# The recurrent mixer of a two-layer trunk: an order given by hand on a grid of twelve products, gated tiles through DRAM

## The chip, the cores and the metric

The kernel runs on one core of one Trainium2 chip. The metric is the device time of one execution in microseconds; of three runs the median is told. The engines go by TensorE (PE), VectorE (DVE), ScalarE (ACT), GpSimd (POOL) and SyncE (SP, whose queue issues most of the DMAs).

## The reference, cut to what matters

Two layers over 1024 frames of width 1024, fp32. Layer 0 is the one that the change touches: a recurrent mixer and its residual.

```python
def recurrent_mixer(hn, w_in, conv_w, conv_b, gate_a_w, ..., lam, w_out):
    z = hn @ w_in                                   # 1024 -> 2 x 1408
    gate, xr = jnp.split(z, 2, axis=-1)
    xr = causal_depthwise_conv(xr, conv_w, conv_b)  # width 4
    y = rg_lru(xr, ...)                             # 16 blocks of 88
    return (y * jax.nn.gelu(gate)) @ w_out          # 1408 -> 1024

# rg_lru, per block of 88 channels:
r = sigmoid(x @ w_a + b_a);  i = sigmoid(x @ w_x + b_x)
log_a = -8 * r * softplus(-lam);  a = exp(log_a)
h[t] = a[t] * h[t-1] + sqrt(1 - a[t]**2) * (i * x)[t]
```

Behind it come a squared-ReLU MLP, one shared key and value, chunked attention and a second MLP. Ahead of each product stands an RMS norm with a scale and shift that are computed from a condition vector (the modulation columns).

## The kernel before, in words

Every fp32 product is made of three: operands are split into a high half (ACT copies to fp32r) and a low half (DVE subtracts), and `mm3` (L272) issues high x high, high x low, low x high into one PSUM bank of 128x512. There are eight banks, taken in turn, and the frames go in two halves of 512. A product below is the whole sum into one bank: 24 matmuls of a unit of w_in, 3 for a gate of a block, 9 or 12 for one of W_out.

`Stream` (L66 to L244) brings the weights. It has one list of items in the order of use; `load` (L129) issues their DMAs on SP into a ring of seven tiles `ws`, `step` (L171) splits them into `wh` (L185, ACT) and `wl` (L189, DVE), and `done` gives them back. An item "u" is no weight but rows for a modulation column (L306, DVE). When `timed` is set, as it is in the MLPs alone, the low halves are put on a list and issued by `flush`.

The mixer has 11 channel tiles t of 128 (1408 in all) and 16 blocks b of 88, so that a block may lie across two tiles and `_done(t)` are the blocks that tile t completes. For each tile there are:

- a unit of w_in for the gate: 48 matmuls, Gelu on ACT (`gate_out`, L675);
- a unit of w_in for the channel: 48 matmuls, two ACT copies out of PSUM (`xr_out`, L680), the convolution as three DVE steps (`conv`, L691), and copies on SP that gather the blocks (L697);
- for each block `split_x` (high L278 on ACT, low L279 on DVE) and `lru`: 12 matmuls, four Sigmoids (L728), Tanh (L735), Sqrt (L737), Exp (L739), each with ACT table loads, DVE steps (L741 to L745), the scan (L746) and copies on SP to the tile `ym` (L750);
- the product with the gate (L709), and later the split of the gated tile into the moving operand of W_out (`split_yg`, L754).

W_out goes in three chunks c of 3, 4 and 4 gated tiles. `chunk2` (L562) makes the two products e of a unit j and half; an eviction on DVE (L571) adds them to the residual h. In the last chunk `tail` (L611) first does all first halves, then the second halves, and among these the norm of the first half for the MLP: squares (L450 on ACT, L451 on DVE), their sums over channels and 1/sqrt (`mm`), the broadcast (`bc`) and the modulation `mod` (L512 on DVE for several channel tiles, then L515 and L523 on ACT for each, and the low, L526, on DVE). Its eight results are the moving operands of the MLP's first products.

What sets the order: the opening (L761 to L862, the norm and the first three units) and each MLP stand in `tc.manual_schedule()`, so that each engine has the order of the code. All of the mixer between them (L865 to L962) is placed by the scheduler with its own estimate of times. Each engine works through its queue in order, and the queue of SP does so too: a DMA that waits for its source or for a free `ws` holds all behind it.

Of the kernel before, what the change touches and what calls it, by code (L numbers as in the profile page):

```python
# [65 lines left out]
class Stream:  # L66
# [8 lines left out]
    def __init__(self, nc, slot, wh, ws):  # L75
        self.nc, self.slot, self.wh, self.ws, self.ns = nc, slot, wh, ws, 7
        self.items = []
        self.loaded = self.raw = self.ring = self.pos = self.now = 0
        self.queue = {"p": [], "w": [], "a": [], "u": []}
        self.live = {"w": 0, "a": 0, "u": 0}  # L80
        self.cap = {"w": 8, "a": 0, "u": 3}

        self.lag = {"p": 4, "w": 0, "a": 2, "u": 4}
        self.hold = None
        self.timed = False
        self.los = []

    def item(self, loads, parts, to="w", rows=128, raw=True, after=None, use=None):

        it = dict(loads=loads, parts=parts, to=to, rows=rows, raw=raw, after=after, use=use,
                  n=len(self.items), at=0, op=[], left=1 if use else len(parts), need=[],
                  cost=sum(1 if one else 2 for _, _, one in parts))
        self.items.append(it)
        self.queue[to].append(it)
        return it
# [31 lines left out]
    def load(self, most=None):  # L129
        while self.loaded < (len(self.items) if self.hold is None else self.hold):  # L130
            it = self.items[self.loaded]
            if most is not None and it["n"] >= most:
                return
            if it["raw"]:
# [36 lines left out]
    def step(self, it):  # L171
        if it["use"]:
            it["use"](it["need"][0]["st"] if it["raw"] is None else it["st"])
        else:
# [13 lines left out]
            def low():  # L188
# [3 lines left out]
                it["hi"], it["lo"] = it["op"][0]  # L192

# [5 lines left out]
        it["left"] -= 1  # L199
        if not it["left"]:  # L200
            if it["raw"]:
                self.raw -= 1
                self.ring -= it["ring"]
            elif it["raw"] is False:
                self.live["u"] -= 1
# [42 lines left out]
def trunk(ctx: ExitStack, tc: tile.TileContext, I, out, dbg=None, stop=None):  # L248
# [92 lines left out]
    for t in range(12):  # L341
        if t < NT:
            for u in (t, 11 + t) if t < NT - 1 else (11 + t, t):
                ws.add(I["w_in"][u], 1024)
        some(2 if 2 < t < 7 else 0)
        if 1 < t < NT:
            for b in _done(t - 1) if t > 2 else (0, 1):
                if b % 4 == 0:
                    ws.add(I["gates"][b // 4], 8 * BLK)
    for c in range(3):  # L350
        kn = 4 if c else 3
        for j in range(4):
# [209 lines left out]
    def chunk2(it, kn, j, half, gh, gl, g, h):  # L562

        for e in range(2):
            m = 2 * j + e
            ps = bank()
            for k in range(kn):
                c = slice(k * 256 + e * 128, k * 256 + e * 128 + 128)
                mm3(ps, it["hi"][:, c], it["lo"][:, c], gh[k][:, hs(half)], gl[k][:, hs(half)],
                    k == 0, k == kn - 1)  # L570
            V.scalar_tensor_tensor(out=h[m][:, hs(half)], in0=ps, scalar=g[:, m : m + 1],  # L571
                                   in1=h[m][:, hs(half)], op0=ALU.mult, op1=ALU.add)
        return [2 * j, 2 * j + 1]

# [73 lines left out]

    xt = [slot() for _ in range(KD)]
# [23 lines left out]
    xc, xb, yg, ym, xraw = {}, {}, {}, {}, {}  # L673

    def gate_out(t, half, ps):  # L675
        if half == 0:
            yg[t] = slot()
        A_.activation(out=yg[t][:, hs(half)], in_=ps, func=AF.Gelu_apprx_tanh)

    def xr_out(t, half, ps):  # L680

        if half == 0:
            xraw[t], xc[t] = slot(), slot()
        A_.activation(out=xraw[t][:, hs(half)], in_=ps, func=AF.Copy)
        A_.activation(out=xc[t][:, hs(half)], in_=ps, func=AF.Identity,
                      scale=vc("cw", 3 * NT + t), bias=vc("cb", t))

    def conv(t):
        xr, y = xraw.pop(t), xc[t]
        for d in (1, 2, 3):  # L690
            V.scalar_tensor_tensor(out=y[:, d:], in0=xr[:, : S - d],  # L691
                                   scalar=vc("cw", (3 - d) * NT + t), in1=y[:, d:],
                                   op0=ALU.mult, op1=ALU.add)
        for b in _done(t):
            x = slot()
            for u, ps, bs in _pieces(b):
                nc.sync.dma_start(x[bs], xc[u][ps])  # L697
            xb[b] = x

    def split_x(b):  # L700
        hi, lo = slot(F32R), slot(F32R)
        split(xb[b][:BLK], hi[:BLK], lo[:BLK])
        xb[b] = (xb[b], hi, lo)

    late = []

    def flush(us):
        for u in us:
            V.tensor_tensor(out=yg[u], in0=yg[u], in1=ym[u], op=ALU.mult)  # L709

    gunit = [None]

    def lru(bs):

        R = {}
        for b in bs:
            if b % 4 == 0:
                gunit[0] = ws.next()
            it = gunit[0]
            x, xh, xl = (a[:BLK] for a in xb.pop(b))  # L720
            r, i_ = slot()[:BLK], slot()[:BLK]
            for gi, (dst, bias) in enumerate(((r, "gab"), (i_, "gxb"))):
                o = ((b % 4) * 2 + gi) * BLK
                w, wl = it["hi"][:BLK, o : o + BLK], it["lo"][:BLK, o : o + BLK]
                for half in range(2):
                    ps = bank()[:BLK]
                    mm3(ps, w, wl, xh[:, hs(half)], xl[:, hs(half)], True, True)
                    A_.activation(out=dst[:, hs(half)], in_=ps, func=AF.Sigmoid,  # L728
                                  bias=vc(bias, b)[:BLK])
            if b % 4 == 3:  # L730
                ws.done(it)
            R[b] = (r, i_, x, slot()[:BLK], slot()[:BLK])

        for b, (r, i_, x, tau, v) in R.items():
            A_.activation(out=tau, in_=r, func=AF.Tanh, scale=n4[:BLK, b : b + 1])  # L735
        for b, (r, i_, x, tau, v) in R.items():
            A_.activation(out=v, in_=tau, func=AF.Sqrt)  # L737
        for b, (r, i_, x, tau, v) in R.items():
            A_.activation(out=r, in_=r, func=AF.Exp, scale=n8[:BLK, b : b + 1])  # L739
        for b, (r, i_, x, tau, v) in R.items():  # L740
            V.scalar_tensor_tensor(out=v, in0=r, scalar=1.0, in1=v, op0=ALU.add, op1=ALU.mult)  # L741
            V.scalar_tensor_tensor(out=r, in0=r, scalar=1.0, in1=tau, op0=ALU.add, op1=ALU.mult)
            V.tensor_scalar(out=r, in0=r, scalar1=-1.0, scalar2=1.0, op0=ALU.mult, op1=ALU.add)
            V.tensor_tensor(out=i_, in0=i_, in1=x, op=ALU.mult)
            V.tensor_tensor(out=v, in0=v, in1=i_, op=ALU.mult)  # L745
            V.tensor_tensor_scan(out=tau, data0=r, data1=v, initial=0.0, op0=ALU.mult, op1=ALU.add)  # L746
            for u, ps, bs in _pieces(b):
                if u not in ym:
                    ym[u] = slot()
                nc.sync.dma_start(ym[u][ps], tau[bs])  # L750
                if ps.stop == 128:
                    late.append(u)

    def split_yg(k):  # L754
        a, b = slot(F32R), slot(F32R)
        split(yg[k], a, b)
        return a, b

    with tc.manual_schedule():  # L761
        n1 = Norm(xt, aa[:, 0:8], mods[0][:, 0:8])
        for k in range(KD):
            n1.sq(k, hs(0))
        sgm = slot()
        A_.activation(out=sgm, in_=cb, func=AF.Sigmoid)

        def ada_k(k):
            for j in (1, 0):
                ada_use(mods[0][:, j * 8 + k : j * 8 + k + 1], vc("ab0", j * 8 + k))(st.pop(0))  # L770
            gain(0, mods[0], 1, vc("n1g0", k), k, 1)

        def sq_b(*ks):
            for k in ks:
                n1.sq(k, hs(1))

        def normed(half, *ks):
            for k in ks:
                V.tensor_tensor(out=xt[k][:, hs(half)], in0=xt[k][:, hs(half)],
                                in1=n1.r[:, hs(half)], op=ALU.mult)  # L780

        def moded(k, half):
            if n1.hh[k] is None:
                n1.hh[k], n1.hl[k] = slot(F32R), slot(F32R)
            t, hi = (a[k][:, hs(half)] for a in (xt, n1.hh))
            A_.activation(out=t, in_=t, func=AF.Identity, scale=n1.a[:, k : k + 1],
                          bias=n1.sh[:, k : k + 1])
            A_.activation(out=hi, in_=t, func=AF.Copy)

        def lows(k, half):  # L790
            t, hi, lo = (a[k][:, hs(half)] for a in (xt, n1.hh, n1.hl))
# [841 lines left out]
```

## Time and profile before

| what | value |
|---|---|
| median of three runs | 2452.64 us (2448.2 to 2452.74) |
| the profiled execution's own time | 2450.6 us |
| its span | 2448.8 us |
| mean granted TensorE clock | 0.978 |
| busy: PE, DVE, ACT, POOL | 2304.2, 1759.7, 1258.3, 370.8 us |
| DMA | 351.91 MB, 144 GB/s on the mean |

The opening ends at about 78 us and the mixer at about 527 us of the span; MLP 0 begins there. Rows of the timeline are: start and duration in us, engine, line of the source, operation, out<-in, shape, and in brackets the idle time ahead of it with what ended it. Rows of groups have the busy time, the mean in ns of one, and the idle time before.

### The profile page before, as it was taken

How to read it: one execution, taken by the hardware profiler on the slowest of the kernel's cores; microseconds unless marked ns; L12 is line 12 of the kernel's file. 1: busy time of each engine (PE TensorE's matmuls, PEld its weight loads, DVE VectorE, ACT ScalarE, POOL GpSimd, SP SyncE). 2: the span in 40 equal slices, each digit the busy share in tenths (PEclk: the TensorE clock that was granted, in tenths of full speed). 3: DMA queues.
4: the chain of work that ended last, by engine and by line, in shares of the span. 5: the costliest groups of instructions: out<-in, count | busy, mean ns of one | idle time of the engine just before them, and what ended most of it. 6: DMA issues, size and time to landing. Idle time of an engine off the chain costs nothing.

```text
span 2448.8 us, 31664 instructions
## 1 busy us (share of the span) xinstructions
PE 2304.2 (94%) x11740; PEld 1941.3 (79%) x11740; DVE 1759.7 (72%) x2586; ACT 1258.3 (51%) x2054; POOL 370.8 (15%) x367
## 2 busy tenths in 40 slices
PE   5989887999999989999999999999999999999999
PEld 3767665777777867888899998998877888778887
DVE  7777777778777687778575466999367656777875
ACT  5577765356444553344343216999156555633442
POOL 0000000000000013332000026886000000023322
PEclk9989887999999999999999999999999999999999
DMA  8422355224566685546343300002413444774543
GB/s 299 129 76 81 113 157 193 64 78 156 207 217 215 233 294 185 155 142 200 114 145 123 113 5 12 10 19 80 142 48 125 156 175 177 259 260 145 159 144 141
DMA packets 138058, 351.91 MB, mean 144 GB/s; under 512 B 14160, under 2 KB 16336, under 8 KB 137904
## 3 DMA queue, kind: packets, MB, share of 16 engines
q1 hardware_dynamic: 114080, 278.45, 35.2%
q10 hardware_dynamic: 23824, 71.44, 7.6%
q8 instruction: 92, 1.51, 0.3%
q14 instruction: 62, 0.51, 0.1%
HBM read 254.42 MB, written 83.89 MB: 138 GB/s over the span
## 4 chain that ended last, share of the span: by engine, by line
PE 55%; DVE 17%; ACT 14%; DMA 8%; issue 5%; POOL 1%; SPq 0%; ACTq 0%; DVEq 0%; POOLq 0%
PE b L274 17%; PE b L275 17%; PE b L273 17%; DMA ws<-in_w_dram 2%; ACT wh L185 2%; DMA ws<-in_ada_dram 2%; DVE wl L189 2%; DVE s L306 2%; DMA hid<-s 1%; PE b L1439 1%; ACT s L1409 1%; DVE s L189 1%; POOL ws L121 1%; DVE ws L121 1%; ACT s L278 1%
## 5 line engine op out<-in xcount | busy, mean ns | idle before, releaser
L273 PE MATMUL b<-s,wh 128*128 128x512 f32 x2532 | 999.3, 398 | 57.4 <-DVE s L1101 15.3
L274 PE MATMUL b<-s,wh 128*128 128x512 f32 x2532 | 1003.3, 397 | 41.1 <-DVE s L279 37.6
L275 PE MATMUL b<-s,wl 128*128 128x512 f32 (+1 forms) x2296 | 909.0, 396 | 6.3 <-DVE wl L189 6.3
L273 PEld LDWEIGHTS b<-s,wh 128*128 128x128 f32 x2532 | 480.1, 190 | 184.8 <-DVE s L1079 19.6
L274 PEld LDWEIGHTS b<-s,wh 128*128 128x128 f32 x2532 | 482.2, 190 | 150.8 <-DVE s L279 41.5
L275 PEld LDWEIGHTS b<-s,wl 128*128 128x128 f32 (+1 forms) x2296 | 437.4, 191 | 105.2 <-DVE wl L189 8.5
L185 ACT ACTIVATE wh<-ws 128x1024 fp32r<-128x1024 f32 (+1 forms) x302 | 290.7, 971 | 428.6 <-POOL ws L121 263.3
L189 DVE TENSOR_TENSOR wl<-ws,wh 128x1024 fp32r<-128x1024 f32 (+1 forms) x249 | 305.3, 1228 | 149.4 <-ACT wh L185 147.1
L121 POOL TENSOR_TENSOR ws<-ws 128x512 f32<-128x512 f32 x21 | 28.2, 1341 | 1592.0 <-DMA ws<-in_w_dram 1093.9
L1101 DVE SCALAR_TENSOR_TENSOR s<-b,mod,s 128x512 f32<-128x512 f32 x221 | 164.8, 746 | 86.6 <-PE b L275 86.0
L275 PE MATMUL b<-wh,s 128*128 128x256 f32 x768 | 216.3, 285 | 3.5 <-DVE s L491 3.3
L273 PE MATMUL b<-wh,s 128*128 128x256 f32 x768 | 218.1, 286 | 0.9 <-ACT s L490 0.9
L274 PE MATMUL b<-wl,s 128*128 128x256 f32 x768 | 217.7, 285 | 0.0
L189 DVE TENSOR_TENSOR s<-ws,s 128x512 fp32r<-128x512 f32 x262 | 210.4, 818 | 1.4 <-ACT s L185 1.4
L185 ACT ACTIVATE s<-ws 128x512 fp32r<-128x512 f32 x262 | 152.2, 619 | 40.8 <-DMA ws<-hid 17.7
L1015 ACT ACTIVATE s<-s 128x512 f32<-128x512 f32 x84 | 53.0, 631 | 217.0 <-DVE s L1079 189.8
L275 PEld LDWEIGHTS b<-wh,s 128*128 128x128 f32 x768 | 147.6, 194 | 4.3 <-DVE s L491 4.3
L306 DVE CUSTOM_DVE_ANT_0 ws<-ws,cb,vec 128x1024 f32<-128x1024 f32 x64 | 81.8, 1282 | 95.3 <-DMA ws<-in_ada_dram 95.2
L273 PEld LDWEIGHTS b<-wh,s 128*128 128x128 f32 x768 | 148.6, 194 | 1.7 <-ACT s L490 1.4
L274 PEld LDWEIGHTS b<-wl,s 128*128 128x128 f32 x768 | 148.7, 194 | 0.4 <-issue 0.2
L1079 DVE TENSOR_TENSOR s<-s,b 128x512 f32<-128x512 f32 x84 | 57.1, 683 | 89.5 <-PE b L275 64.5
L1208 ACT ACTIVATE s<-b 128x256 f32<-128x256 f32 x96 | 31.3, 383 | 129.2 <-PE b L275 114.6
(166 smaller groups left out, 3079.8 us busy)
## 6 DMA issues: line engine op xcount, KB each, us to landing
hid<-s ACTq DMA_DIRECT2D x128, 512.0 KB
ws<-hid SPq DMA_DIRECT2D x118, 512.0 KB
ws<-in_w_dram SPq DMA_DIRECT2D x220, 256.0 KB
ws<-in_ada_dram SPq DMA_DIRECT2D x64, 512.0 KB
s<-in_ada_dram SPq DMA_DIRECT2D x32, 512.0 KB
ws<-in_w_in_dram SPq DMA_DIRECT2D x22, 512.0 KB
hsp<-s SPq DMA_DIRECT2D x32, 256.0 KB
s<-in_kvada_dram SPq DMA_DIRECT2D x16, 512.0 KB
```

The source lines that it names most:

```text
L121: eng.tensor_tensor(out=out, in0=in0, in1=in1, op=op)
L185: self.nc.scalar.activation(out=hi[:rows, :n], in_=src, func=AF.Copy)
L189: self.nc.vector.tensor_tensor(out=lo[:rows, :n], in0=src, in1=hi[:rows, :n].bitcast(F32), op=ALU.subtract)
L273: PE.matmul(ps, ah, bh, start=start, stop=False, skip_group_check=more)
L274: PE.matmul(ps, ah, bl, start=False, stop=False, skip_group_check=more)
L275: return PE.matmul(ps, al, bh, start=False, stop=stop, skip_group_check=more).ins
L278: A_.activation(out=hi, in_=src, func=AF.Copy)
L306: V.tensor_tensor_reduce(out=t, in0=t, in1=cb, op0=ALU.mult, op1=ALU.add, scale=1.0, scalar=bias, accum_out=dst)
L1015: A_.activation(out=t, in_=t if src is None else src, func=AF.Relu)
L1079: V.tensor_tensor(out=t, in0=t, in1=ps, op=ALU.add)
L1101: V.scalar_tensor_tensor(out=t, in0=ps, scalar=g2[:, m : m + 1], in1=t, op0=ALU.mult, op1=ALU.add)
L1208: A_.activation(out=d, in_=ps[:, :, e * 128 : (e + 1) * 128], func=AF.Copy)
```

## The change

The mixer's instructions get the order of the code: `tc.manual_schedule()` is entered before the norm of the opening and left only after MLP 0. The code is rewritten to give that order. In this section line numbers are those of the kernel after, unless before is said; elsewhere they are those of before.

- A grid. The function `tick()` stands after each 12 matmuls of w_in and W_out and after each block's gates. It runs what `at(d, f)` has put off by d ticks, then issues up to two low halves of weights and lets `Stream` load and split.
- Order of units. Channel tile t + 1 and the gates' products of tile t come ahead of the gate unit of t: xr(0), xr(1), gate(0) in the opening, then xr(2), gate(1), blocks 0 and 1, and for t from 3 on xr(t), blocks of t - 1, gate(t - 1); at the end gate(9), blocks 14 and 15, gate(10).
- Steps behind a channel tile. The convolution at once, the copies one tick later, the high half of the split three and the low half four ticks later. Behind a block's gates: i * x one tick later, Tanh after the last block of the tile, Sqrt and Exp two ticks later, scans 4 + 2n ticks later, their copies (L933), then the gated product.
- Gated tiles are written to DRAM (`ygd`, 11 stores of 512 KB, L940) and are items of `Stream` that come back (11 loads) and are split in halves of 512 as any operand. A load is held until its store is three ticks old.
- W_out's loops are written in the order j, half, e (`chunk`, evictions L1024); in chunk 2 the norm is spread over the second half: `mm` after unit 1's first product, `bc` after unit 2's first, and the modulation in pieces of 3, 3 and 2 channel tiles after the last three products.
- The softplus constants n4 and n8 of the recurrence are computed ahead of the opening's norm instead of behind it.
- In the first loop of an MLP's opening the fourth weight runs one k behind the other three. `early` keeps the MLP's release of a raw tile where it was; in the mixer a raw tile is given back only when its last low is issued.

```diff
+    order = ExitStack()
+    order.enter_context(tc.manual_schedule())
...
+    def tick(most=2):
+        while True:
+            due = [x for x in jobs if x[0] <= now[0]]
+            if not due:
+                break
+            for x in due:
+                jobs.remove(x)
+                x[1](*x[2])
+        ws.flush(most)
+        now[0] += 1
+        ws.now += 1
+        ws.pump()
...
+    def conved(t):
+        conv(t)
+        at(1, copies, t)
+        at(3, split_hi, t)
+        at(4, split_lo, t)
...
+    def recur(bs):
+        for b in bs:
+            gates(b)
+        tanhs(bs)
+        at(2, roots, bs)
+        for n, b in enumerate(bs):
+            at(4 + 2 * n, scan, b)
...
+    xr(2)
+    gate(1)
+    recur(_done(0) + _done(1))
+    for t in range(3, NT):
+        xr(t)
+        recur(_done(t - 1))
+        if t < NT - 1:
+            gate(t - 1)
+    gate(NT - 2)
+    recur(_done(NT - 1))
...
+    ws.cap["a"] = 6
+    gate(NT - 1)
+    load_h(4)
...
+            for j in range(4):
+                for e in range(2):
+                    chunk(j, 1, e)
+                    if (j, e) == (1, 0):
+                        n2.mm(0)
+                    elif (j, e) == (2, 0):
+                        n2.bc(0)
+                    elif j > 1:
+                        n2.mod(0, {(2, 1): (0, 1, 2), (3, 0): (3, 4, 5), (3, 1): (6, 7)}[j, e])
+                    tick(4)
+                at(1, ws.done, its[j])
...
-        for k in range(KD):
+        for k in range(KD + 1):
             for f, it in enumerate(its):
-                plain(ps[f], it, k, 0)
+                if 0 <= k - (f == 3) < KD:
+                    plain(ps[f], it, k - (f == 3), 0)
             head(k, nrm)
```

Two places in the order of the engines. First DVE at the end of W_out, in the kernel before. `L571` is an eviction, `L512` a normalised half (of channel tiles 0 to 7), `L526` a low of it, `L189` a weight's low for the MLP.

```order
L512 SCALAR_TENSOR_TENSOR s_2326<-s_2326,aa,s_2456 128x512
L512 SCALAR_TENSOR_TENSOR s_2328<-s_2328,aa,s_2456 128x512
L512 SCALAR_TENSOR_TENSOR s_2444<-s_2444,aa,s_2456 128x512
L512 SCALAR_TENSOR_TENSOR s_2446<-s_2446,aa,s_2456 128x512
L512 SCALAR_TENSOR_TENSOR s_2448<-s_2448,aa,s_2456 128x512
L512 SCALAR_TENSOR_TENSOR s_2450<-s_2450,aa,s_2456 128x512
L512 SCALAR_TENSOR_TENSOR s_2452<-s_2452,aa,s_2456 128x512
L512 SCALAR_TENSOR_TENSOR s_2454<-s_2454,aa,s_2456 128x512
L571 SCALAR_TENSOR_TENSOR s_2448<-b_3337,mod_82,s_2448 128x512
L526 TENSOR_TENSOR s_3330<-s_2326,s_3330 128x512
```

The eight normalised halves stand together, and evictions, squares' sums and lows come behind them. The same place of DVE in the kernel after; `L1024` is the eviction, `L542` the normalised half, `L481` adds a square that ACT makes, `L556` is the low, `L195` a weight's low.

```order
L542 SCALAR_TENSOR_TENSOR s_2593<-s_2593,aa,s_2536 128x512
L481 TENSOR_TENSOR s_3158<-s_3158,s_3450 128x512
L556 TENSOR_TENSOR s_3441<-s_2534,s_3441 128x512
L556 TENSOR_TENSOR s_3444<-s_2591,s_3444 128x512
L556 TENSOR_TENSOR s_3447<-s_2593,s_3447 128x512
L1024 SCALAR_TENSOR_TENSOR s_2635<-b_3456,mod_82,s_2635 128x512
L542 SCALAR_TENSOR_TENSOR s_2633<-s_2633,aa,s_2536 128x512
L542 SCALAR_TENSOR_TENSOR s_2635<-s_2635,aa,s_2536 128x512
L481 TENSOR_TENSOR s_3158<-s_3158,s_3482 128x512
L556 TENSOR_TENSOR s_3473<-s_2633,s_3473 128x512
L556 TENSOR_TENSOR s_3476<-s_2635,s_3476 128x512
L195 TENSOR_TENSOR wl_3479<-ws_2970,wh_3478 128x1024
```

Each piece now has its normalised halves, then a square's sum, its lows, and in the end a weight's low; the next piece stands behind all that. ACT at the same place after: `L545` and `L553` are the two steps for a channel tile, `L480` a square, `L191` the high half of the MLP's third weight.

```order
L545 ACTIVATE s_2591<-s_2591,mod_82 128x512
L553 ACTIVATE s_3444<-s_2591 128x512
L545 ACTIVATE s_2593<-s_2593,mod_82 128x512
L553 ACTIVATE s_3447<-s_2593 128x512
L480 ACTIVATE s_3450<-s_2593 128x512
L545 ACTIVATE s_2633<-s_2633,mod_82 128x512
L553 ACTIVATE s_3473<-s_2633 128x512
L545 ACTIVATE s_2635<-s_2635,mod_82 128x512
L553 ACTIVATE s_3476<-s_2635 128x512
L191 ACTIVATE wh_3478<-ws_2970 128x1024
L480 ACTIVATE s_3482<-s_2633 128x512
```

The square that a sum of DVE needs stands behind the steps of a piece, and the weight's high half behind the last piece. Second, SP in the kernel after, at the last channel tile: `L156` loads rows or weights into the ring, `L860` gathers blocks 14 and 15, `L940` stores a gated tile.

```order
L940 DMA ygd<-s_1985 128x1024
L156 DMA ws_2286<-in_ada_dram 128x1024
L156 DMA ws_2289<-in_ada_dram 128x1024
L860 DMA s_2306<-s_2004 48x1024
L860 DMA s_2306<-s_2213 40x1024
L860 DMA s_2309<-s_2213 88x1024
L156 DMA ws_2361<-in_w_out_dram 128x768
```

And in the kernel before, where `L697` gathers, and `L908` loads the residual.

```order
L152 DMA ws_2653<-in_ada_dram 128x1024
L152 DMA ws_2710<-in_ada_dram 128x1024
L152 DMA ws_2712<-in_ada_dram 128x1024
L697 DMA s_2321<-s_2276 40x1024
L697 DMA s_2324<-s_2276 88x1024
L908 DMA s_2326<-in_xT_dram 128x1024
L908 DMA s_2328<-in_xT_dram 128x1024
```

In both, the last copies stand behind loads into the ring; after, the store of a gated tile is among them.

556 lines of the change are left out of this document (297 added, 259 removed).

## The prediction

> **What bounds the kernel now.** I read first the windows of the trace over the mixer (the stretch from the end of its opening, 78 us, to the start of MLP 0, 527 us), then the waits of TensorE (PE), then the timelines at the longest waits. The change ends where MLP 0 has begun, so the rest of the span is only carried along. The columns below are the stretch and its length, then the busy time (and instructions) of PE, its weight loads, VectorE (DVE), ScalarE (ACT) and GpSimd, the granted PE clock, the DMA share and GB/s.
>
> ```profile
> 78.00:527.00 449.00, 402.91 (x1648) 316.10 (x1646) 336.15 (x367) 274.72 (x323) 0.00 (x0) 0.91 0.38 118
> 139.70:148.80 9.10, 0.00 (x0) 0.00 (x0) 5.42 (x6) 4.17 (x6) 0.00 (x0) 0.61 0.42 125
> 148.80:158.80 10.00, 9.97 (x24) 6.58 (x25) 6.81 (x6) 6.51 (x9) 0.00 (x0) 0.50 0.18 48
> 158.80:163.80 5.00, 5.00 (x24) 4.12 (x23) 2.36 (x2) 4.97 (x6) 0.00 (x0) 1.00 0.36 108
> 385.30:390.90 5.60, 5.55 (x13) 4.40 (x14) 2.27 (x2) 0.00 (x0) 0.00 (x0) 0.50 0.92 334
> 460.00:527.00 67.00, 66.89 (x296) 54.51 (x295) 46.07 (x69) 23.96 (x36) 0.00 (x0) 1.00 0.25 86
> 530.40:534.20 3.80, 3.75 (x10) 2.98 (x11) 3.00 (x5) 0.00 (x0) 0.00 (x0) 0.55 0.39 138
> ```
>
> In 460 to 527 PE never stops and runs at full clock: 67.00 / 296 = 0.2263 us a matmul, the pace. The 1648 matmuls of the mixer would take 372.9 us at it; they take 449.0. So 76.1 us are lost: 449.00 - 402.91 = 46.1 with PE idle, and about 30 in which PE works at a reduced clock. The second loss follows the first: after the 9.10 us without PE the clock is 0.50 for 10.00 us, in which 24 matmuls pass, where the next 24 pass in 5.00. That stretch alone costs 5.0 us beside its idle 9.1. DVE (336 of 449) and ACT (275 of 449) have room on average: the mixer is a matter of order. Who PE waits for (in total, times, longest):
>
> ```profile
> PE b L274 <- DVE s L279: 37.6, 8, 9.2
> ```
> ```profile
> 385.35 0.80 PE L274 MATMUL b<-s,wh 128*128 128x512 f32 x1 [7.64 <-DVE s L279]
> 527.34 0.50 PE L273 MATMUL b<-s,wh 128*128 128x512 f32 x1 [0.45 <-ACT wh L185]
> 530.45 0.50 PE L275 MATMUL b<-s,wl 128*128 128x512 f32 x1 [2.37 <-DVE wl L189]
> ```
>
> Nearly all of it is one wait: the gates' products (and at 385.35 W_out's) stand in PE's queue for the low half of a split (L279) of a tile that has only just left the convolution. The path of such a tile at the worst place, DVE then SP:
>
> ```profile
> 379.17 1.28 DVE L691 SCALAR_TENSOR_TENSOR s<-s,vec,s 128x1021 f32<-128x1021 f32 x1
> ```
> ```profile
> 380.51 1.70 SPq L697 DMA_DIRECT2D s<-s  x2
> ```
>
> The convolution ends at 380.45, SP issues the two copies at 380.51, and PE goes on at 385.35: 4.9 us from conv to the first gate product, even where nothing stands ahead of the copies.
>
> **The change part by part.**
> *The tile loop.* Products now follow a grid of twelve, and the gates of a tile come nine ticks (9 x 12 x 0.2263 = 24.4 us) after its convolution, because a gate unit (four ticks) and the next channel unit stand between. The copies are due one tick, the high half three and the low half four ticks (10.9 us) after the convolution is issued; on DVE at most a scan (6.6 by the rows below), a gated tile (1.2) and a modulation column (1.3) stand between, which makes 17 to 21 us. So the regular tiles cost PE nothing. What hides them is those nine ticks. This removes the 37.6 us wait and most of the slow clock, all but three places and the MLP's start. Rows for the prices:
>
> ```profile
> L189 DVE TENSOR_TENSOR wl<-ws,wh 128x1024 fp32r<-128x1024 f32 x68 | 83.0, 1221 | 38.4 <-ACT wh L185 38.3
> L185 ACT ACTIVATE wh<-ws 128x1024 fp32r<-128x1024 f32 x68 | 71.4, 1051 | 61.2 <-PE b L274 47.1 <-issue 11.0 <-DVE ws L121 2.0
> L306 DVE CUSTOM_DVE_ANT_0 ws<-ws,cb,vec 128x1024 f32<-128x1024 f32 x32 | 40.7, 1280 | 22.8 <-DMA ws<-in_ada_dram 22.7
> L746 DVE TENSOR_TENSOR_SCAN s<-s,s 88x1024 f32<-88x1024 f32 x16 | 36.3, 2280 | 0.2
> L571 DVE SCALAR_TENSOR_TENSOR s<-b,mod,s 128x512 f32<-128x512 f32 x48 | 34.8, 746 | 18.2 <-PE b L275 16.6 <-DMA s<-in_xT_dram 1.5
> L737 ACT ACT_TABLE_LOAD x16 | 20.5, 1283 | 0.3
> L739 ACT ACTIVATE s<-s,sp 88x1024 f32<-88x1024 f32 x16 | 18.4, 1153 | 0.2
> L737 ACT ACTIVATE s<-s 88x1024 f32<-88x1024 f32 x16 | 17.0, 1063 | 0.2
> L741 DVE SCALAR_TENSOR_TENSOR s<-s,s 88x1024 f32<-88x1024 f32 x16 | 19.5, 1220 | 33.7 <-ACT s L739 28.5 <-ACT s L737 5.1
> L743 DVE TENSOR_SCALAR s<-s 88x1024 f32<-88x1024 f32 x16 | 10.7, 678 | 0.0
> L476 PE MATMUL b<-s,ones 128*128 128x512 f32 x8 | 6.3, 880 | 3.4 <-DVE s L470 3.4
> L879 DVE TENSOR_SCALAR sp<-sp 128x16 f32<-128x16 f32 x7 | 1.2, 173 | 0.2
> ```
>
> *The opening.* It keeps its steps. Its last low in before:
>
> ```profile
> 74.21 0.69 DVE L792 TENSOR_TENSOR s<-s,s 128x512 fp32r<-128x512 f32 x1 [1.56 <-ACT s L788]
> ```
>
> Nine matmuls follow that low: 74.90 + 9 x 0.2263 = 76.9. The softplus chain now stands ahead of the first squares on DVE: about 24 operations of 0.173 us, 4.1 at most, 0 if they are done before x lands. I take 1.4, so 78.3.
> *The products.* From there 1613 matmuls stand in the new order before the first of two products that are left when the normed halves are wanted (W_out's last chunk, unit 2, second half, e = 1): 365.0 us. The norm's sums and broadcast take 1.3 (the broadcast 0.88). That makes 444.6 without a wait.
> *First wait: blocks 0 and 1.* Only here no gate unit follows the recurrence. The roots of both blocks (two table loads, two square roots, two exponentials: 2 x (1.283 + 1.063 + 1.153) = 7.0 us on ACT) stand ahead of the second half of channel tile 3, whose bank the gates of block 3 need. PE has some 2 to 3 us of other work, so 4 to 5 idle, plus about 3 of slow clock: 8 (0 to 12).
> *Second wait: blocks 14 and 15.* Here the gates come five ticks (13.6 us) after the last convolution, not nine. DVE then has the scan of a block ahead (1.220 x 2 + 0.678 + 1.22 + 2.280 = 6.6), a gated tile, a modulation column (1.28) and the three convolution steps, and SP has two weight loads ahead of the copies, which wait for slots that DVE frees. After that come the 4.9 us. I get 5.3 us idle (0 to 9, the worst wait of before) and 5 of slow clock: 10 (0 to 14).
> *Third wait: W_out's first chunk.* DVE has 47 us of work in its queue in these sixteen products (sixteen evictions of 0.75, most of two scans, fourteen modulation columns of 1.28, lows of loaded tiles and weights), PE 16 x 9 x 0.2263 = 32.6. Eight banks let PE run ahead by at most eight products, 16 us, and what is left of the 14.7 us lies between 0 and 14. Row by row I get 6.6 and 1.5 for the loads of gated tiles that were stored shortly before: 8. The 22 added transfers cost nothing else that I see.
> *The MLP's start.* In before the eight normalising operations stand together on DVE and ACT is fed ahead; in after they come in three pieces of 3, 3 and 2, and behind each DVE stands in its queue at the sum of a square that ACT does only after that piece's pairs. The prices:
>
> ```profile
> 515.88 5.39 DVE L512 SCALAR_TENSOR_TENSOR s<-s,aa,s 128x512 f32<-128x512 f32 x8
> 526.77 1.28 DVE L526 TENSOR_TENSOR s<-s,s 128x512 fp32r<-128x512 f32 x2
> 529.17 1.22 DVE L189 TENSOR_TENSOR wl<-ws,wh 128x1024 fp32r<-128x1024 f32 x1
> ```
> ```profile
> 541.26 0.73 ACT L515 ACTIVATE s<-s,mod 128x512 f32<-128x512 f32 x1 [0.82 <-DVE s L512]
> 542.02 0.63 ACT L523 ACTIVATE s<-s 128x512 fp32r<-128x512 f32 x1
> 542.56 0.71 ACT L515 ACTIVATE s<-s,mod 128x512 f32<-128x512 f32 x1
> ```
>
> A DVE step takes 0.67 (normalise, evict), 0.64 (low, sum), 1.22 (weight low). A pair on ACT takes 542.56 - 541.26 = 1.30, a square 0.63, a weight split 1.05. Counted from the end of that product: first piece, evict and one step 1.3, three pairs to 5.2, weight split 6.2, square 6.8, then sum, three lows and weight low: 10.6. Second piece: evict and step 12.0, three pairs 15.9, square 16.5, sum and three lows 19.0. Third: evict and step 20.4, two pairs 23.0, the third weight's split 24.0, square 24.7, sum, two lows and that weight's low: 27.8. PE has two products (5.4 us) and a few matmuls (1.4 us) to do, and then waits for the third weight: about 20 us idle, of which the split's own place is 16. Before waits 2.37 there, and loses 3.80 x 0.45 = 1.7 after it. After 20 us of idle I take the 5.0 of the 10 us stretch: 3.2 more.
> *Sum.* 444.6 + 8 + 10 + 8 + 27.8 = 498.4 at the point that before reaches at 530.45: 32.0 sooner, less 3.2: 28.8. From there both orders are the same. The profiled execution took 2450.6 (span 2448.8), two below the median of the runs (2452.64), so 2450.6 - 28.8 = 2421.8, said as 2422.
>
> **A rule weighed.** In this trace the reduced clock lasts 10.00 us after a wait of 9.1, 5.60 after 7.64, and 3.80 after 2.37. The Trainium skill (TensorE: Matmul & The Clock Gate, Part 1: The HAM clock gate) says that full clock comes back after one busy window of about 3.4 us. The trace agrees at 530.4 and contradicts it at 148.8; by the page the time would be that of rival D.
>
> **The rivals.**
> *A: the MLP's start stays covered*, if ACT and DVE run ahead of PE there. The third low would come about 8 us after that product (two products and a wait like before's 2.37), not 27.8: 19.8 less, and no 3.2: 2399. For it speaks that before passes the place with 2.8 us of waits; against it that each step waits in its queue for the one named. 0.17.
> *B: the waits only move*: upper bounds at the first three (12 + 14 + 14 = 40 in place of 26) and 10 us more in the loop's regular tiles, from DVE: about 2446, and up to 2451 with the opening's 4.1. 0.08.
> *C, slower: SP's one queue makes every tile late.* Copies stand behind weight loads that wait for ring slots; the ring is freed by DVE and ACT, which are a tile behind. Where a tile's way from conv to gates exceeds its 24.4 us, PE stops as at 148.8. It decides from 28.8 / 9 = 3.2 us lost at each of the nine tiles. With idle 5.3 and slow clock 5 at each it gives 2421.8 + 93 = 2515, with half of that 2468. For it speaks that the last tile's copies stand behind two such loads; against it that the sum of a tile's steps, 17 to 21 us, is under 24.4. 0.13.
> *D: every reduced clock is as short as at 530.4*, 1.7 lost, in place of my 3, 5 and 5: 1.3 + 3.3 + 3.2 = 7.8 less, 2414. 0.03, since two of the rows above last longer.
> That the change does nothing can be set aside: the orders of the engines differ throughout the mixer.
>
> **How the numbers follow.** My sum has 0.59, and its own range by the bounds of its unknown costs is 2408 to 2440. The range reaches from A with a few us of room, 2394, to the upper end of B, 2452; outside lie C and a little at the lower end. Under 0.2% (4.9 us) a measurement can't tell the kernels apart. Faster: my sum, A, D and 0.03 of B, 0.82; same: the rest of B, 0.05; slower: C, 0.13.
>
> **What would show it.** Right: no wait of the gates' products for the low of their input in the regular tiles; the granted clock at full from about 120 to 350; a wait of PE of 12 to 20 us at the first use of the MLP's third weight, at about 475 to 500, with DVE's sums waiting for ACT's squares just before it; three shorter waits, for a bank in tile 3, for the last blocks' lows, and for evictions in W_out's first chunk. Wrong: a PE wait at every tile with SP's copies late (C); no long wait at the MLP's start (A); W_out's first chunk losing over 14 us, or DVE busy without a gap through the whole loop (B).

## The result, and the profile after

The changed kernel takes 2492.31 us (median of four runs, 2491.07 to 2495.7) against 2450.42 before (four runs too, of which the table above has the first three): a ratio of 1.0174, interval 1.0156 to 1.0192. It is slower by 42 us, where the prediction had 28.8 us faster. The profiled execution took 2495.7 us with a span of 2493.6.

The point that was forecast for 498.4 us (the third weight's low at the MLP's start, 530.45 before) comes at 576.97, 78.6 later. From there to the end 1917 us pass, as before (1918). So all of the loss lies in the mixer. The waits of PE in the first 850 us of the kernel after (line of PE, line that it waited for, total, times, longest); L866 is the high half of a block's split on ACT, L839 the Gelu, L898 the Sigmoids, L1024 W_out's evictions on DVE:

```profile
PE b L285 <- ACT s L839: 20.9, 7, 4.7
...
PE b L285 <- ACT s L866: 20.3, 4, 14.6
PE b L285 <- DVE s L1024: 12.9, 4, 5.5
PE b L285 <- ACT wh L191: 12.6, 1, 12.6
...
PE b L285 <- ACT s L898: 6.3, 2, 5.3
...
PE b L286 <- DVE s L873: 2.9, 4, 0.8
```

The old wait, products for the low half of a split (37.6 us), is gone: that low (L873) is waited for 2.9 us in all. Waits for ACT have come in its place, at every tile, and most of them for a Gelu, from which PE needs no more than two emptied banks. The windows of the kernel after (stretch and length, then busy time and count of PE, its weight loads, DVE, ACT, POOL, then the granted clock, DMA share, GB/s):

```profile
78.00:160.00 82.00, 73.31 (x308) 56.85 (x306) 57.25 (x56) 57.72 (x70) 0.00 (x0) 0.96 0.41 121
160.00:362.00 202.00, 175.36 (x686) 134.35 (x687) 130.76 (x109) 124.34 (x149) 0.00 (x0) 0.89 0.30 90
374.00:389.00 15.00, 0.39 (x3) 0.01 (x1) 7.33 (x10) 1.12 (x2) 0.00 (x0) 0.68 0.66 196
389.00:403.20 14.20, 13.67 (x32) 8.79 (x33) 13.06 (x13) 14.07 (x16) 0.00 (x0) 0.50 0.22 66
425.00:460.00 35.00, 21.96 (x77) 16.20 (x76) 31.15 (x36) 2.35 (x3) 0.00 (x0) 0.87 0.75 240
```

At the pace of 0.2263 us a matmul, the regular tiles (160 to 362) lose 202.0 - 686 x 0.2263 = 46.8 us, of which 26.6 are idle and 20 reduced clock (the granted clock is 0.89). They were forecast to lose nothing. Why, is read on ACT and DVE at one tile. The timeline of ACT in the kernel after:

```profile
237.80 1.06 ACT L191 ACTIVATE wh<-ws 128x1024 fp32r<-128x1024 f32 x1
252.84 1.06 ACT L866 ACTIVATE s<-s 88x1024 fp32r<-88x1024 f32 x1 [13.97 <-DMA s<-s]
254.90 1.06 ACT L866 ACTIVATE s<-s 88x1024 fp32r<-88x1024 f32 x1 [1.00 <-DMA s<-s]
255.97 1.28 ACT L915 ACT_TABLE_LOAD   x1
257.27 1.06 ACT L915 ACTIVATE s<-s 88x1024 f32<-88x1024 f32 x1
```

ACT stands for 14 us at the high half, for copies that have not landed. Behind it in the queue stand the roots (L915, L918) of the blocks before, whose inputs are long there, and behind these the Gelu that PE waits for. The same stretch of DVE and of SP's queue:

```profile
260.80 1.22 DVE L922 SCALAR_TENSOR_TENSOR s<-s,s 88x1024 f32<-88x1024 f32 x1 [3.60 <-ACT s L918]
265.17 2.29 DVE L926 TENSOR_TENSOR_SCAN s<-s,s 88x1024 f32<-88x1024 f32 x1
273.68 1.23 DVE L939 TENSOR_TENSOR s<-s,s 128x1024 f32<-128x1024 f32 x1 [5.10 <-DMA s<-s]
274.82 3.92 DVE L852 SCALAR_TENSOR_TENSOR s<-s,vec,s 128x1023 f32<-128x1023 f32 x3
```
```profile
280.29 1.46 SPq L860 DMA_DIRECT2D s<-s  x2
```

DVE waits for the roots, scans, waits for the scan's copies (5.10), multiplies with the gate, and only then does the next convolution (L852, ending at 278.7). SP issues its copies at 280.29, and the next high half starts on ACT at 285.26. That is a ring: high half, roots, scan, gated tile, convolution, copies, next high half, through three queues that each keep their order. Its time is read from the high halves: 218.9, 252.8, 285.3, 319.1, 350.8, some 33 us a tile. PE's work for a tile is 96 matmuls of two units and 12 for each of 16/11 blocks, 25.7 us at the pace. One turn, from 252.84 to 285.26, is made of 8.0 us on ACT until the roots are done, 6.7 on DVE to the end of the scan, 6.2 until its copies have landed, 5.1 for the gated tile and the convolution, and 6.5 until the next split's copies have landed. The Trainium skill (TensorE: Matmul & The Clock Gate, Part 1: The HAM clock gate) says that ACT and DVE work strictly in order; the 13.97 us with ready work behind agree.

The MLP's start came as worked out. PE and DVE of the kernel after there:

```profile
557.75 0.50 PE L286 MATMUL b<-s,wh 128*128 128x512 f32 x1 [2.61 <-DVE s L556]
573.38 0.80 PE L285 MATMUL b<-s,wh 128*128 128x512 f32 x1 [12.60 <-ACT wh L191]
576.97 0.79 PE L287 MATMUL b<-s,wl 128*128 128x512 f32 x1 [2.36 <-DVE wl L195]
```
```profile
549.52 0.75 DVE L1024 SCALAR_TENSOR_TENSOR s<-b,mod,s 128x512 f32<-128x512 f32 x1 [0.89 <-PE b L287]
556.40 0.69 DVE L481 TENSOR_TENSOR s<-s,s 128x512 f32<-128x512 f32 x1 [4.15 <-ACT s L480]
565.88 0.69 DVE L481 TENSOR_TENSOR s<-s,s 128x512 f32<-128x512 f32 x1 [3.19 <-ACT s L480]
573.88 0.69 DVE L481 TENSOR_TENSOR s<-s,s 128x512 f32<-128x512 f32 x1 [3.53 <-ACT s L480]
```

From the eviction at 549.52 to the third weight's low at 576.97 it is 27.4 us (27.8 forecast), with DVE at each of the three pieces in front of the sum of a square that ACT has not made.

### The profile page after: what moved, and what is told of

It is laid out like the page before. It is cut to its first block, busy times and chain, and to the rows that moved or that the text cites. A ratio compares the mean times of both kernels' runs of the same rounds, so it can differ in the third digit from the quotient of the medians.

```text
span 2493.6 us, 31716 instructions
## 1 busy us (share of the span) xinstructions
PE 2317.0 (93%) x11740; PEld 1948.7 (78%) x11740; DVE 1761.6 (71%) x2596; ACT 1243.6 (50%) x2055; POOL 370.2 (15%) x367
## 4 chain that ended last, share of the span: by engine, by line
PE 52%; DVE 17%; ACT 13%; DMA 10%; issue 6%; POOL 1%; SPq 1%; ACTq 0%; DVEq 0%; POOLq 0%
PE b L285 16%; PE b L287 16%; PE b L286 16%; DMA s<-s 3%; DVE wl L195 3%; DMA ws<-in_w_dram 2%; ACT wh L191 2%; DMA ws<-in_ada_dram 2%; DVE s L318 2%; DVE s L195 2%; PE b L1551 1%; ACT s L1521 1%; ACT s L553 1%; DVE ws L123 1%; ACT s L290 1%
## 5 line engine op out<-in xcount | busy, mean ns | idle before, releaser
L285 PE MATMUL b<-s,wh 128*128 128x512 f32 (+1 forms) x2532 | 1016.3, 401 | 118.2 <-ACT s L839 20.9
L286 PE MATMUL b<-s,wh 128*128 128x512 f32 (+1 forms) x2532 | 1006.0, 397 | 9.3 <-DVE s L744 3.5
L285 PEld LDWEIGHTS b<-s,wh 128*128 128x128 f32 (+1 forms) x2532 | 483.8, 191 | 251.3 <-ACT s L839 24.8
L286 PEld LDWEIGHTS b<-s,wh 128*128 128x128 f32 (+1 forms) x2532 | 484.6, 191 | 117.7 <-issue 5.2
L191 ACT ACTIVATE wh<-ws 128x1024 fp32r<-128x1024 f32 (+2 forms) x302 | 290.1, 970 | 392.7 <-POOL ws L123 261.8
L195 DVE TENSOR_TENSOR wl<-ws,wh 128x1024 fp32r<-128x1024 f32 (+2 forms) x249 | 303.8, 1223 | 151.1 <-ACT wh L191 149.1
L123 POOL TENSOR_TENSOR ws<-ws 128x512 f32<-128x512 f32 x21 | 27.8, 1322 | 1639.5 <-DMA s<-hsp 952.4
L195 DVE TENSOR_TENSOR s<-ws,s 128x512 fp32r<-128x512 f32 x284 | 225.0, 809 | 1.4 <-ACT s L191 1.4
L191 ACT ACTIVATE s<-ws 128x512 fp32r<-128x512 f32 x284 | 164.1, 618 | 57.8 <-DMA ws<-hid 17.7
```

Source lines behind the costliest of these rows:

```text
L123: eng.tensor_tensor(out=out, in0=in0, in1=in1, op=op)
L191: self.nc.scalar.activation(out=hi[:rows, :n], in_=src, func=AF.Copy)
L195: self.nc.vector.tensor_tensor(out=lo[:rows, :n], in0=src, in1=hi[:rows, :n].bitcast(F32), op=ALU.subtract)
L285: PE.matmul(ps, ah, bh, start=start, stop=False, skip_group_check=more)
L286: PE.matmul(ps, ah, bl, start=False, stop=False, skip_group_check=more)
```

## The experiments

Theory A: the ring above. Theory B, the prediction's rival C: SP's one queue sends each tile's copies late. Times are set beside the 2492.31 of the kernel after; the ratios are to the kernel before the change, timed on the same chip. That kernel took 2450.42 us beside the kernel after, and 2453.77 (the first four runs below), 2451.81 (the next four) and 2454.92 us (the last three) beside these. So a difference of two times carries up to some 4 us of chip; what the ratios give stands in brackets. Where a period is told, it is half the distance between the high halves of every second tile.

**The split put off.**

```diff
-        at(3, split_hi, t)
-        at(4, split_lo, t)
+        d = 6 if 1 < t < NT - 1 else 3
+        at(d, split_hi, t)
+        at(d + 1, split_lo, t)
```

> In tiles 2 to 9 the high half of the split (ACT) and its low half (DVE) are put off from three and four ticks after the convolution to six and seven, so that on ACT they stand behind the roots of the blocks before. Theory A, a ring of queues: ACT stands at the high half until the copies land, the roots stand behind it, the scans behind the roots, the next convolution behind the scans and the gated tile, and its copies behind that; the ring takes about 33 us a tile (high halves at 218.9, 252.8, 285.3, 319.1) where PE needs about 26. Then this cuts the ring: the waits of 160 to 362 us (26 us idle) and the slow clock behind them go for the greater part, the 14.6 us wait ahead of the last blocks becomes 5 to 10, and the time is 2435 to 2455. Theory B, SP's one queue: copies leave late behind loads; nothing of that is changed here, so 2485 to 2495.

2452.36 us, 40 less (44 by the ratios); ratio 0.9996 (0.9985 to 1.0008). Two windows and two waits of this run:

```profile
78.00:532.70 454.70, 400.22 (x1657) 316.14 (x1655) 340.97 (x365) 266.70 (x330) 0.00 (x0) 0.91 0.45 142
170.50:337.70 167.20, 165.14 (x726) 132.30 (x724) 135.06 (x114) 123.68 (x146) 0.00 (x0) 1.00 0.39 116
```
```profile
PE b L286 <- DVE s L873: 11.3, 2, 10.8
PE b L285 <- ACT s L866: 8.2, 1, 8.2
```

From 170.5 to 337.7 PE runs at full clock and is idle for 2 of 167 us. Nothing was changed but the place of two short operations in two queues: the copies still leave from SP and still take their time. The high halves come at 207.9, 259.8 and 312.7 for every second tile: the period is 26 us, PE's own. A holds, B does not. Of the tile loop's waits two longer ones are left: one new, 10.8 us at tile 3, whose low now stands on DVE behind scans, and 8.2 at the last blocks (14.6 in the kernel after). W_out's waits for DVE (12.5 us in all) and the 12.5 us at the MLP's start are as they were.

**The gated tile put off.**

```diff
-                at(2, gated, u)
+                at(6, gated, u)
```

> The product with the gate is put off from two ticks after its tile's last copy to six, so that on DVE it stands behind the next convolution, not ahead of it. Theory A: this takes from the ring the copies to ym that DVE stands for (4 to 5 us a tile) and the product (1.2): the period falls from 33 to about 27 us, and the time to 2450 to 2465. Theory B: the copies ahead of the split leave SP as before, 2485 to 2495.

2466.09 us, 26 less (31 by the ratios); ratio 1.0049 (1.0033 to 1.0065). A second cut of the same ring, on another engine, and just short of what A expected. The period is 29.5 us (high halves at 209.2, 268.6, 327.2) and not 27: its turns are 26 and 33 us long alternately, the long one where the scans of two blocks stand ahead of the convolution. The roots still stand behind the high half, for which ACT waits 11.88 us at 242.0.

**The copies on another queue.**

```diff
-                nc.sync.dma_start(x[bs], xc[u][ps])
+                nc.gpsimd.dma_start(x[bs], xc[u][ps])
```

> The copies that gather the blocks (26 of them) are issued from the queue of POOL, which has nothing else in the mixer, instead of SP's. Theory A: at most tiles SP issues them 1.2 to 2.4 us after the convolution's end already, at tiles 1 and 3 some 12 and 9 us; only that is won, 10 to 25 us in all: 2466 to 2482. Theory B: the waits of the regular tiles go with SP's queue: 2430 to 2450.

2477.73 us, 15 less (19 by the ratios); ratio 1.0097 (1.0082 to 1.0112). From the convolution's end to the high half it is now 3 to 4 us in the tiles from 4 on, where it was 6 to 8, and the period falls from 33 to 30 us (high halves at 212.7, 274.2, 333.5). So SP's queue is one link of the ring, worth 15 to 19 of the 42 us, and not the whole. Its part shows most in the kernel after at tile 3, where the convolution ends at 134.7 and the copies leave at 143.71, behind loads that wait for free raw tiles:

```profile
142.09 0.33 SPq L156 DMA_DIRECT2D ws<-in_w_in_dram  x1
143.29 0.32 SPq L156 DMA_DIRECT2D ws<-in_gates_dram  x1
143.71 1.45 SPq L860 DMA_DIRECT2D s<-s  x2
```

**The modulation earlier and in one piece.**

```diff
-                    if (j, e) == (1, 0):
+                    if (j, e) == (0, 1):
                         n2.mm(0)
-                    elif (j, e) == (2, 0):
+                    elif (j, e) == (1, 1):
                         n2.bc(0)
-                    elif j > 1:
-                        n2.mod(0, {(2, 1): (0, 1, 2), (3, 0): (3, 4, 5), (3, 1): (6, 7)}[j, e])
+                    elif (j, e) == (2, 0):
+                        n2.mod(0, range(KD))
```

> At the end of the mixer the norm's sums, its broadcast and the modulation stand one product earlier, and the modulation in one piece of eight instead of 3, 3 and 2. By the chain of ACT and DVE that the prediction worked out (there 27.8 us from the end of W_out's product for unit 2, e = 1, to the third weight's low; 27.4 in the profile after), this order gives about 20: 7 us sooner, with a little less slow clock, 2482 to 2487. If the wait is for something else there (the weight's load), no change: 2489 to 2495.

2487.43 us, 5 less (9 by the ratios); ratio 1.0136 (1.0119 to 1.0152), the time just above what was expected. The third weight's low comes at 568.70, 8.3 us sooner, where the chain gave 7. So the order of ACT and DVE does set this wait. But one square's sum now waits for all eight pairs instead of three, so the place is still a chain of two engines.

**The gate unit ahead of the last blocks**, on top of the split put off.

```diff
     gate(NT - 2)
+    ws.cap["a"] = 6
+    gate(NT - 1)
     recur(_done(NT - 1))
...
-    ws.cap["a"] = 6
-    gate(NT - 1)
     load_h(4)
```

> The late split of tiles 2 to 9, and besides the gate unit of tile 10 stands ahead of blocks 14 and 15 instead of behind them, so that these blocks' products have nine ticks behind their convolution as all others. With the late split alone PE still waits 8.2 us there for the high half, and runs at a reduced clock after it: 2452. If that wait is a matter of five ticks against nine, it goes: 2438 to 2447. If it moves into W_out's first chunk, where the two blocks' scans then stand later on DVE, the time stays at 2449 to 2456.

2442.15 us, 10 less than with the late split alone (8 by the ratios); ratio 0.9963 (0.9952 to 0.9975). PE waits for no high half any more, so five ticks against nine it was. But ACT still stands for 14.45 us at the last high half (342.25), and the Gelu of tile 10 stands behind it: PE waits for that 6.8 us at 355. The wait for tile 3's low is left too, 11.6 us.

**All of it in one.** The late split for tiles 4 to 9, the gate unit ahead, the modulation in one piece from (1, 1) on, the softplus chain behind the opening. Shown in part; the rest is as in the runs of the single steps.

```diff
+        d = 6 if 3 < t < NT - 1 else 3
...
+                    elif (j, e) == (1, 1):
+                        n2.bc(0)
                     tick(4)
+                    if (j, e) == (1, 1):
+                        n2.mod(0, range(KD))
```

> All in one: the late split (tiles 4 to 9 alone, since the run with it had a new wait of 10.8 us for the low of tile 3), the gate unit of tile 10 ahead of blocks 14 and 15, the modulation in one piece of eight two products earlier and behind the tick's square, and the softplus chain behind the opening. If the waits are the ones named and add up: 2452 less 10 (tile 3), 8 (last blocks), 9 (MLP's start) and 3 (opening), 2415 to 2435, faster than the kernel before the change. If they only move on to one another: 2440 to 2455.

2442.3 us; ratio 0.9964 (0.995 to 0.9979). This missed: no better than the run before it. Leaving tiles 2 and 3 at three ticks brought their ring back, among it the wait for the Sigmoids behind tile 2's high halves (7.4 us), and W_out's waits for DVE stayed at 12.2 us. At the wait for tile 10's Gelu this run is 6.6 us behind the one before it (361.73 against 355.13), at the third weight's low 0.9 ahead (521.01 against 521.94): what the modulation won at the end, the tile loop had lost. The pieces did not add up.

**The softplus chain back.** The 18 lines from `sp = ...` to `n8` go behind the opening again.

> The softplus chain alone goes back behind the opening. PE's longest wait in the opening was 12.0 us before and 15.1 after, so if the chain ahead of the first squares on DVE is the reason: 3 us less, 2487 to 2491. If the chain is done before x lands, as the prediction's lower bound had it: no difference, 2491 to 2494.

2495.2 us; ratio 1.0181 (1.0159 to 1.0204), no faster than the kernel after. PE's longest wait in the opening falls from 15.1 to 11.9 us, so the chain is its reason, and at the MLP's start the run is 2.7 us ahead (574.25 against 576.97), but from there to the end it took 1921 us in place of 1917, and the run as a whole does not show the gain. Inconclusive: 3 us is about what separates one chip's runs from another's here.

**The mixer left to the scheduler.** The code is that of after; only the manual order is left at the opening's end and taken up again for the MLP.

```diff
+    order.close()
     ws.timed = True
     ws.lag["w"] = 2
...
-            if l:
-                given.enter_context(tc.manual_schedule())
+            given.enter_context(tc.manual_schedule())
...
-        if l == 0:
-            order.close()
```

> The rewritten code of the mixer as it is, but the manual order is left at the end of the opening and taken up again for the MLP, so that the scheduler places the mixer's instructions. If the given order of the queues is what costs (theory A) and not the rewritten work (the trip through DRAM, the order of units, splits in halves), the time falls to 2440 to 2475. If the rewritten work costs, or the scheduler builds the same ring, 2480 to 2500.

2438.32 us, 54 less than after (54 by the ratios too); ratio 0.9953 (0.9938 to 0.9969). The rewritten work (channels ahead of gates, the trip through DRAM, splits in halves) is not what costs; it is even a little faster than before. The given order is what costs. In W_out, whose products run from about 390 us on in this run, PE waits for no eviction at all. The same stretch of time as above, here in the second chunk:

```profile
425.00:460.00 35.00, 35.00 (x156) 28.82 (x154) 35.00 (x52) 8.87 (x12) 0.00 (x0) 1.00 0.84 290
```

DVE is busy without a gap there (35.00 of 35.00), and still PE loses nothing.

**W_out and the MLP's start left to the scheduler**, the tile loop as in after (`order.close()` ahead of W_out; the MLP takes up its own order as in the run before).

> The kernel after with its given order up to the last gate unit; from W_out's first chunk to the MLP the scheduler places the instructions. Theory: the loss has two parts, the ring of the tile loop (about 40 us by the run with the late split) and the given order at the end (W_out's first chunk 12.9 us and the MLP's start 18.7 us of waits, and their slow clock). Then the tile loop stays as it was and the end loses no more than 5 to 8: 2455 to 2470. If the tile loop alone were the cause and the end only the place where its lateness shows: 2485 to 2495.

2466.38 us, 26 less (29 by the ratios); ratio 1.0054 (1.0034 to 1.0073). The end of the mixer has its own 26 us, beside the ring's 40; the high halves of this run still come some 33 us apart.

**Loop given, end scheduled.** Both repairs and the gate unit ahead.

```diff
+        d = (3, 3, 6, 5, 6, 6, 6, 6, 6, 6, 3)[t]
+        at(d, split_hi, t)
+        at(d + 1, split_lo, t)
...
+    ws.cap["a"] = 6
+    gate(NT - 1)
     recur(_done(NT - 1))
+    order.close()
     h = []
...
-    ws.cap["a"] = 6
-    gate(NT - 1)
```

> Tile loop in the given order with the late split (six and seven ticks; for tile 3 five and six, since its low stood behind scans) and the gate unit of tile 10 ahead of the last blocks; W_out and the MLP's start placed by the scheduler. If both repairs add up: 2442 less 10 to 15 for W_out, 10 to 15 for the MLP's start and 5 to 10 for tile 3, 2402 to 2420. If W_out takes back what the loop wins, because the last two scans and the gated tiles meet it there: 2425 to 2440.

2422.0 us, 70 less than after (75 by the ratios); ratio 0.9866 (0.9849 to 0.9883): 1.3% faster than the kernel before, the best of the study, if just short of what was expected. The parts nearly add up (40 + 26 + 10 = 76). One wait of 8.8 us is new, for a weight's high half in W_out; those of 6.7 us for tile 10's Gelu and 5.7 for lows are left. A window of its loop:

```profile
196.40:348.50 152.10, 152.10 (x669) 121.95 (x667) 116.81 (x102) 109.35 (x128) 0.00 (x0) 1.00 0.38 113
```

**Scheduler, and the gate unit ahead.** The run with the scheduler, with the gate unit of tile 10 ahead of the last blocks.

> The whole mixer placed by the scheduler (2438), with the gate unit of tile 10 ahead of blocks 14 and 15. Its largest wait was 12.0 us for the high half of the last blocks, with a reduced clock for 12 us behind it. If that goes with the four ticks more: 2420 to 2430. If the scheduler or W_out's DVE work takes it back: 2433 to 2442.

2443.42 us; ratio 0.9949 (0.9929 to 0.9968), no better than 2438. The 12.0 us wait for the last high half is 0.3 now, and 0.8 for its low, but waits of 5.0 us for a Gelu (at 374) and 7.6 for a weight's high half (at 458) have come. Under the scheduler the wait moved.

## Why the prediction was wrong

*What bounds the kernel.* The loss of before, 76 us of order rather than of work, was read rightly: with another order of the rewritten work, 33 us of it were won. The wait for the low of a split was named rightly too, and it is gone. But what it waited for was misread. At the longest such wait of before, ACT, then DVE, then PE:

```profile
139.25 1.04 ACT L278 ACTIVATE s<-s 88x1024 fp32r<-88x1024 f32 x1
```
```profile
146.42 1.22 DVE L709 TENSOR_TENSOR s<-s,s 128x1024 f32<-128x1024 f32 x1 [3.65 <-DMA s<-s]
147.56 1.21 DVE L279 TENSOR_TENSOR s<-s,s 88x1024 fp32r<-88x1024 f32 x1
```
```profile
148.83 0.73 PE L274 MATMUL b<-s,wh 88*88 88x512 f32 x1 [9.15 <-DVE s L279]
```

The tile had not only just left the convolution: its copies had landed by 139.25, both high halves were done at 140.29, and the low stood 7.3 us on DVE behind scans and a gated tile that waited for its own copies. At 266.51, 332.02 and 372.60 it is the same, with 4.9, 6.2 and 6.4 us between. So what stands ahead in a queue was the matter in before already. Nor is there a way of 4.9 us from the convolution to the gates. At 385.35 PE waits for the low of a gated tile (128 rows, its high half done by 372.42); the blocks whose copies left at 380.51 are split from 404.43 on. In the kernel after, 5.0 to 7.2 us pass from the issue of the copies to the high half alone.

*The tile loop: this step failed.* The prediction said that the regular tiles cost PE nothing, because nine ticks hide the way from the convolution to the gates. It followed one tile along its own chain, 17 to 21 us, and counted what stands ahead of it on DVE. It did not ask what stands behind the waiting operation on its engine. ACT's high half waits for the copies, and the roots of the blocks before, the Gelu and the next tile's copies out of PSUM stand behind it. The roots then hold DVE, and DVE holds the next convolution. So the tile's chain is no way of 20 us but a ring of 33 us, and its period, not its delay, is what has to lie under PE's 26 us. By windows it cost 46.8 us from 160 to 362 where 0 stood. Two cuts at two places (40 and 26 us, periods of 26 and 29.5 us) show it. Of the prediction's signs, the full clock from 120 to 350 did not come (0.89).

*The opening.* 78.3 forecast; the last low ends at 77.5, which makes 79.5 with the nine matmuls. The softplus chain is worth 3 us of wait and not 1.4.

*First wait, 8.* From 78 to 160 the loss is 82.0 - 308 x 0.2263 = 12.3, but not for the reason given. The largest part is the wait of 5.3 us for the Sigmoids of blocks 0 and 1 at 110.85, which stand behind tile 2's high halves, with the slow clock after it; the roots of these blocks cost 1.1 us at 132.8, and 2.4 us before 160 are the first wait for a Gelu.

*Second wait, 10.* From 374 to 403.2 only 35 matmuls pass: 29.2 - 7.9 = 21.3 lost. The wait was 14.6 us, not 5.3, in part since the convolution before it was late by the ring (with the ring cut it is 8.2), in part since the way from the issue of the copies to the gates was taken as 4.9 us and is 8.4 here (380.64 to 388.99). The five ticks were the right reason, as the gate unit ahead shows.

*Third wait, 8.* From 425 to 460 the loss is 35.0 - 77 x 0.2263 = 17.6. DVE's queue is the reason, as forecast, but it started with a wait that the sum did not have:

```profile
424.73 0.75 DVE L1024 SCALAR_TENSOR_TENSOR s<-b,mod,s 128x512 f32<-128x512 f32 x1 [8.26 <-DMA s<-in_xT_dram]
```

The first eviction stands for the residual's load, and the scans of the last blocks stand behind it. The estimate of 1.5 us for loads was for the gated tiles; the residual had none. No run loads it earlier, so what this wait is worth by itself is not shown.

*The MLP's start, 27.8.* 27.4, by the chain that was worked out, and not covered: rival A falls. The wait at the third weight was 12.6 us, in the range of the sign.

The terms that came out too small make 1.2 + 4.3 + 46.8 + 11.3 + 9.6 = 73 of the 78.6 us; some 3 us more lie in the stretches between these windows. Rival C had the sign and a size (2468 to 2515), and a queue in order as its mechanism, but the wrong queue: a queue other than SP's can hold a tile as well. SP's own share is 15 to 19 us. Rival B, upper bounds everywhere, was too small.

*Rule weighed, rival D.* After 389.0 the clock stays at 0.50 for 14.20 us in which PE is busy for 13.67. The Trainium skill's one busy window of about 3.4 us (same page and section) does not hold there, so rival D falls; it does hold at 577.0, where it is 3.7 us.

What stays open: whether the waits that are left in the scheduler's version (9.4 us for Sigmoids, 15.2 for high halves) could be cut as well, which was not tried beyond the gate unit, and what sets the length of a stretch of reduced clock.

## What to carry to other kernels

When an order is given by hand, follow for each operation that may wait (above all for a DMA) what stands behind it on its engine, until you come back to where you began: a ring through several queues has a period, and that period has to be under the bound engine's time for one turn. A chain's delay can be hidden by starting early; a ring's period cannot. And put an operation that waits for a transfer behind the ready work of its queue: here three ticks of patience on ACT were worth 40 us. Nor does a wait for an operation tell what that operation waited for: look whether its inputs were long there.

## What the runs showed of the hardware

The reduced clock does not follow from the length of the wait. It lasted 14.2 us after a wait of 14.6, but 3.7 us after 12.6 and 2.4:

```profile
577.00:580.70 3.70, 3.70 (x9) 2.92 (x10) 3.63 (x6) 0.00 (x0) 0.00 (x0) 0.50 0.24 73
```

The long stretches here and before (14.2 and 10.0 us) begin with the gates' products of 88 rows, the short ones with products of 128. In both kernels the stretches that no wait of over 1 us interrupts or ends last 5.7 to 14.4 us where they begin with 88 rows and 3.1 to 5.7 where they begin with 128 (read from the time of a matmul, 0.63 us against 0.39). No run told apart whether that is the reason.

The two or three copies that gather a tile's blocks (88 partitions of 4 KB a block) take 5 to 7 us from the first issue on SP to the operation that they release: 246.31 to 252.84, 280.29 to 285.26, 380.64 to 387.88. From POOL's queue they were no slower: there 3 to 4 us pass from the convolution's end to that operation.
